# Decays by pair of heads, one-pass squares and a longer due time for the substitution in a gated-delta layer

## The chip, the cores and the metric

The kernel runs on one core of one Trainium2 chip. The metric is the device time of one launch in microseconds (us); the time shown is the median of three runs.

## The reference

One inference step through two layers of a streaming encoder, for 1024 prompt frames and 64 frames of a running stream (1088 columns in all, 17 chunks of 64), width 1024, all in fp32. Layer 1 (a gated convolution beside banded attention) is not touched. Layer 2 is a gated DeltaNet with 8 heads of 128: a projection, a causal convolution of width 4 with SiLU on q, k and v, and per head and chunk:

```python
def gdn_chunk(S, q, k, v, g, beta):
    gc = jnp.cumsum(g, axis=1)
    decay = jnp.exp(jnp.where(incl, gct[..., :, None] - gct[..., None, :], -jnp.inf))
    a = jnp.where(strict, bt[..., :, None] * kk * decay, 0.0)     # kk = k k^T
    sol = lax.linalg.triangular_solve(a + eye, rhs, left_side=True, lower=True, unit_diagonal=True)
    u = sol[..., :HD_C] - sol[..., HD_C:] @ S
    o = (q * jnp.exp(gc)) @ S + (q k^T * decay) @ u
    S_new = jnp.exp(g_last) * S + k_dec^T @ u
```

q and k are first divided by their norm (`l2norm`, a sum of squares over 128). S goes from chunk to chunk, so the 17 chunks of a head are a chain. The output is normed per head, multiplied by silu(z) and projected.

## The kernel before

**Tiling.** A projection takes one weight tile of 128 output columns (`w`) and runs over three groups of columns (384, 384, 320). Every fp32 product is made of three matmuls in fp32r, from weights and inputs that were split into a high and a low part: `pjt<-hhi,wlo`, `pjt<-hhi,whi`, `pjt<-hlo,whi`, for each of eight slices of the contraction. Below, a "projection row" is one such matmul. ACT and DVE split the weights (`whi` L164, `wlo` L165) as they come by DMA (`wf`, on SP's queue).

**Layer 2.** The heads go in four pairs p = 0 to 3. `conv_tile` projects and convolves six tiles for a pair (q, k, v). The 17 chunks of a pair come in three batches of 6, 6 and 5 chunks; the twelve batches n = 3p + b each go through five streams of work:

- `prep` (function `prepare`): the decays `E` (`decay`: DVE L902 spreads the running sums `gc` into `An`, a matmul `tr<-An,cst` adds them up across lanes, DVE L907 subtracts, ACT L908 and L909 make exp(-|x|)); transposes of k and q (`tr<-cst,kq`), of which ACT takes squares chunk by chunk with an accumulator (`junk`, L948), ACT copies k (`kt`, L950) and DVE scales it (`kd`, L951); POOL takes the root of the sums (`rk`, L956 and L957), scales `kt` (L961) and masks `E` into `KQD` (L962); matmuls `tr<-kq`, from which DVE makes `An` (L970) and `KQD` (L971); and the diagonal blocks `Af`, which SP's queue writes to DRAM.
- `sub` (`substitute`): SP's queue reads them back as `AL`, and POOL inverts 48 blocks of 16x16 row by row (`px` L996, `AL` L997); SP's queue writes them to DRAM again.
- `inv` (`join`): read as `Xf`, masked by POOL into `X` (L1025), transposed by DVE into `XT` (L1026), and joined to inverses of 64x64 by small matmuls (`tr<-XT,Cb` first, then `tr<-M,X`, `tr<-XT,An`, `tr<-M,X`).
- `wy` (`solve`): `tr<-cst,vt`, `tr<-BD,kt`, `tr<-vr,BD`.
- `scan`: chunk by chunk `ks<-S,kq`, DVE makes `us` (L1145), `su<-us,kd`, DVE makes the new `S` (two instructions, L1159), and `tr<-us,KQD` gives the output, which DVE adds up (`o`, L1114) and ACT squares (L1118). For each four chunks `finish` takes POOL's root (`so`, L1173 and L1174), scales `o` (DVE L1176) and transposes it (`tr<-cst,o`).

All these matmuls and transposes write PSUM tiles named `tr` (two banks), `ks` and `su`. A `tr` bank is free again when its last reader on ACT or DVE is through.

**What sets the order.** TensorE's order is written by the kernel itself: `Order` has a clock of its own, which each matmul moves on by its columns. A stream is a generator; `yield w` says that it is due again w ns later, and of the streams that are due the one with the lowest rank goes on: `scan` 1, `wy` 1.3, `inv` 1.5, `sub` 1.6, `prep` 2, the stream `main` with all projections 5. So projections fill what the others leave. `yield "name"` waits for a stream's end: `main` waits for `scan2` before pair 2 and for `scan5` before pair 3 (two buffers of `kq`), and for the last batch's transposed outputs before tile 6 of the gate. DVE, ACT, POOL and SP are ordered by the compiler's scheduler. Every engine then takes its own list strictly in order.

Of the kernel before, what the change touches and what calls it, by code (L numbers as in the profile page):

```python
# [7 lines left out]
F32 = mybir.dt.float32  # L8
# [7 lines left out]
P = 128  # L16
# [91 lines left out]
class Net:  # L108
# [650 lines left out]
    def odd(self):  # L759
# [16 lines left out]
        def conv(ti, dst, g, ps, prev):  # L776
# [20 lines left out]
            if half:  # L797
                th = k1.tile([P, GMAX + 3], F32, name="th", tag="raw", bufs=3)[:, :n]
                act.activation(ch(th), o, AF.Tanh)
                dve.scalar_tensor_tensor(o, ch(th), 1.0, o, ALU.add, ALU.mult)  # L800
            else:
                act.activation(o, o, AF.Silu)
# [29 lines left out]
        def gate(ti):  # L832
            w = self.take()
            for g, (t0, n) in enumerate(GROUPS):
# [9 lines left out]
                nc.sync.dma_start(oo, od[:, ti, t0:t0 + n])  # L844
                zs = (gp if ti == 7 else k1).tile([P, GMAX + 3], F32, name="zs", tag="raw", bufs=3)[:, :n]
                act.activation(zs, ps[:, :n], AF.Silu)
# [50 lines left out]

        def decay(e, gx, p, c0, m):

            sh = [P, m, 64]  # L900
            gcb = G["gc"][:, p, c0:c0 + m].unsqueeze(2).broadcast_to(sh)
            dve.tensor_tensor(gx, gcb, cst[:, C_ID64:C_ID64 + 64].unsqueeze(1).broadcast_to(sh), ALU.mult)  # L902
            yield 900
            ps = pst("tr")[:, :64 * m]
            self.mm(ps, cst[:, C_BD:C_BD + P], gx.rearrange("p c j -> p (c j)"))
            ps = ps.rearrange("p (c j) -> p c j", j=64)
            dve.tensor_tensor(ps, ps, gcb, ALU.subtract)  # L907
            act.activation(e, ps, AF.Abs)  # L908
            act.activation(e, e, AF.Exp, scale=-1.0)  # L909

# [10 lines left out]
        def prepare(p, b):  # L921
# [10 lines left out]

            E, An, KQD = bt("E", 64), bt("An", 64, 2), bt("KQD", 64, 3)
            yield from decay(E, An, p, c0, nb)
            if b == 0:
                yield 4000
            kd, kt = bt("kd", P, 3), bt("kt", P, 2)
            ss = self.kp.tile([P, 2, NBM], F32, name="ss", tag="ss", bufs=2)[:, :, :nb]
            junk = self.kp.tile([P, P], F32, name="junk", tag="junk", bufs=1)
            for i0 in range(0, nb, 4):  # L940
                m = min(4, nb - i0)
                for a in range(2):
                    ps = pst("tr").rearrange("p (c j) -> p c j", j=P)
                    for i in range(m):
                        c = c0 + i0 + i
                        self.tr(ps[:, i, :], kq[:, a, c].rearrange("p q t -> p (q t)"))
                    for i in range(m):
                        act.activation(junk, ps[:, i, :], AF.Square, accum_out=ss[:, a, i0 + i:i0 + i + 1])  # L948
                    if a == 0:
                        act.copy(out=kt[:, i0:i0 + m, :], in_=ps[:, :m, :])  # L950
                        dve.tensor_tensor(kd[:, i0:i0 + m, :], ps[:, :m, :],  # L951
                                          dec[:, p, c0 + i0:c0 + i0 + m].unsqueeze(2).broadcast_to([P, m, P]), ALU.mult)
                    yield 2160
            sT, sA, kap, rk, eq = (small(x) for x in ("sT", "sA", "kap", "rk", "eq"))
# [29 lines left out]
        def substitute(p, b):  # L984
# [7 lines left out]
            for j in range(1, 15):  # L992
# [5 lines left out]
                if j % 2 == 0:  # L998
                    yield 700
            pool.memset(AL.rearrange("p r j -> p (r j)")[:, 0:256:17], 1.0)  # L1000
# [186 lines left out]

        def add_pair(p):
            for b in range(NB):
                n = NB * p + b  # L1190
# [6 lines left out]
                order.add(f"sub{n}", 1.6, substitute(p, b), [f"prep{n}"] + after("sub", n - 1))  # L1197
                order.add(f"prep{n}", 2, prepare(p, b), ["gates"] + after("prep", n - 1) + after("wy", n - 2) + after("scan", n - 3))

# [133 lines left out]
```

## Time and profile before

| | |
|---|---|
| median of 3 runs | 1436.92 us (1434.3 to 1437.56) |
| profiled execution | 1433.82 us, its span 1432.0 us |
| PE busy | 1362.8 us, 95% of the span |
| DVE, ACT, POOL busy | 58%, 49%, 19% |
| mean granted TensorE clock | 0.986 |

An engine's busy time is the union of its instructions. A busy PE is not a PE at its peak, since a matmul's row is longer than the distance to the next one. In the views a row such as `PE tr L119 <- ACT E L908` means that TensorE's next instruction, which writes or reads a tile `tr`, waited for ACT's instruction at line 908. L119 is the line of the helper that records all matmuls, L124 that of all transposes.

### The profile page before, as it was taken

Reading aid. Unit: us, or ns where it says so; the run is one execution under the profiler, and the core shown is the slowest. Engines: PE = TensorE matmul, PEld = TensorE weight load, DVE = VectorE, ACT = ScalarE, POOL = GpSimd, SP = SyncE. Lnnn points to the kernel's source line nnn. Section 1 sums busy time; section 2 is a strip of 40 time slices with the busy share of each in tenths; the row PEclk is TensorE's granted clock in tenths of the full one; section 3 lists DMA queues with packets and bytes.
Section 4 is the critical chain, followed back from the end, with each engine's and each line's share of the span. In section 5 each row is a group of like instructions: output and inputs, shape, how many; then the busy total and the mean of one; then the engine's idle time right before and its main releaser. Section 6 shows DMA issues by size and latency. Waiting matters only on the chain. (4 is left out here: it accounts for less than half of the span.)

```text
span 1432.0 us, 27829 instructions
## 1 busy us (share of the span) xinstructions
PE 1362.8 (95%) x10600; PEld 1227.5 (86%) x10600; DVE 834.1 (58%) x2232; ACT 696.7 (49%) x1792; POOL 276.0 (19%) x578
## 2 busy tenths in 40 slices
PE   8999999999999999999999988999999989999996
PEld 6989998998999899888987777787878777889995
DVE  7675247237425754778786756667665654433555
ACT  7543345144334455675545463546454635333752
POOL 4000000000100014322151325212412151300122
PEclk9999999999999999999999999999999999999998
DMA  8403111210211164451220212112211232336753
GB/s 267 140 17 90 57 53 45 88 53 22 77 58 53 61 229 151 158 186 38 60 40 19 46 37 52 16 44 45 47 15 42 68 68 60 91 103 206 235 197 123
DMA packets 106917, 123.77 MB, mean 86 GB/s; under 512 B 34512, under 2 KB 73880, under 8 KB 106784
## 3 DMA queue, kind: packets, MB, share of 16 engines
q1 hardware_dynamic: 78992, 99.86, 23.7%
q10 hardware_dynamic: 27792, 22.15, 4.9%
q8 instruction: 83, 1.36, 0.4%
q14 instruction: 50, 0.41, 0.1%
HBM read 95.26 MB, written 29.86 MB: 87 GB/s over the span
## 5 line engine op out<-in xcount | busy, mean ns | idle before, releaser
L119 PE MATMUL pjt<-hhi,wlo 128*128 128x384 f32 (+1 forms) x1768 | 613.9, 347 | 2.3 <-DVE wlo L165 2.3
L119 PE MATMUL pjt<-hhi,whi 128*128 128x384 f32 (+1 forms) x1768 | 582.5, 330 | 8.1 <-ACT whi L164 4.7
L119 PE MATMUL pjt<-hlo,whi 128*128 128x384 f32 (+1 forms) x1768 | 575.2, 329 | 1.1 <-DVE hlo L417 1.1
L119 PEld LDWEIGHTS pjt<-hhi,wlo 128*128 128x128 f32 x1768 | 335.9, 190 | 26.0 <-issue 11.6
L119 PEld LDWEIGHTS pjt<-hhi,whi 128*128 128x128 f32 x1768 | 336.6, 190 | 13.8 <-ACT whi L164 6.0
L119 PEld LDWEIGHTS pjt<-hlo,whi 128*128 128x128 f32 x1768 | 334.5, 190 | 2.0 <-DVE hlo L417 2.0
L165 DVE TENSOR_TENSOR wlo<-wf,whi 128x512 fp32r<-128x512 f32 x222 | 151.8, 709 | 167.6 <-ACT whi L164 162.7
L164 ACT CAST whi<-wf 128x512 fp32r<-128x512 f32 x222 | 130.2, 619 | 163.3 <-PE pjt L119 116.0
L638 ACT ACTIVATE pr<-pr,mx 128x640 f32<-128x640 f32 (+5 forms) x72 | 50.9, 707 | 89.4 <-DVE mx L637 88.8
L796 DVE SCALAR_TENSOR_TENSOR kq<-pjt,par,kq 128x384 f32<-128x384 f32 (+2 forms) x144 | 71.7, 498 | 3.0
L374 POOL TENSOR_TENSOR sqa<-sqa,sq 128x384 f32<-128x384 f32 (+1 forms) x36 | 39.1, 1086 | 137.1 <-ACT sq L371 137.0
L635 DVE CUSTOM_DVE_ANT_0 pr<-sc,bias 128x640 f32<-128x640 f32 (+5 forms) x72 | 48.0, 666 | 26.7 <-PE sc L119 25.9
L599 POOL MEMSET bias<- 64x64 f32 x8 | 1.4, 173 | 320.5 <-DMA bias<-Gd 227.5
L1159 DVE SCALAR_TENSOR_TENSOR S<-S,egl,su 128x128 f32<-128x128 f32 x128 | 39.8, 342 | 37.3 <-PE su L119 37.2
L948 ACT ACTIVATE junk<-tr 128x128 f32<-128x128 f32 x136 | 37.7, 277 | 33.4 <-PE tr L124 27.0
L996 POOL TENSOR_TENSOR px<-AL 48x14 f32<-48x14 f32 (+6 forms) x168 | 45.4, 270 | 33.4 <-DMA AL<-Sd 21.6
L1118 ACT ACTIVATE junk<-o 128x128 f32<-128x128 f32 x68 | 21.0, 309 | 61.4 <-DVE o L1114 55.1
L997 POOL TENSOR_TENSOR AL<-AL,px 48x14 f32<-48x14 f32 (+6 forms) x168 | 47.7, 284 | 11.7
L124 PE MATMUL pt<-cst,pr 128*128 128x128 f32 (+1 forms) x280 | 43.3, 270 | 4.3 <-DVE pr L640 2.9
L119 PE MATMUL pjt<-mhi,whi 128*128 128x384 f32 x128 | 43.0, 336 | 1.2 <-ACT whi L164 1.2
L119 PE MATMUL pjt<-mhi,wlo 128*128 128x384 f32 x128 | 43.0, 336 | 0.1
L119 PE MATMUL ks<-S,kq 128*64 128x128 f32 x512 | 43.0, 288 | 0.0
(252 smaller groups left out, 2107.1 us busy)
## 6 DMA issues: line engine op xcount, KB each, us to landing
wf<-in_w_in SPq DMA_DIRECT2D x128, 256.0 KB, 3.3
wf<-in_w_out SPq DMA_DIRECT2D x96, 256.0 KB, 2.9
mf<-mixd SPq DMA_DIRECT2D x31, 192.0 KB, 4.2
x<-in_x SPq DMA_DIRECT2D x8, 384.0 KB, 6.7
xg<-in_x SPq DMA_DIRECT2D x2, 1536.0 KB
xd<-xg SPq DMA_DIRECT2D x2, 1536.0 KB, 7.3
od<-o ACTq DMA_DIRECT2D x12, 256.0 KB, 2.1
oo<-od SPq DMA_DIRECT2D x16, 192.0 KB
```

Of the source, the lines that this page charges most:

```text
L119: return self.pe.matmul(out, lhsT=lhsT, rhs=rhs, start=start, stop=stop, **k)
L124: return self.pe.transpose(out, in_, self.ident[0:k, 0:k])
L164: self.act.copy(out=hi, in_=x)
L165: (eng or self.dve).tensor_tensor(lo, x, hi.bitcast(F32), ALU.subtract)
L374: pool.tensor_tensor(acc, acc, sq, ALU.add)
L635: dve.tensor_tensor_reduce(out=cut(pr[0:nq, :nk]), in0=sc[0:nq, :nk // nw, :nw], in1=cut(b["bias"][a][0:nq, j0:j0 + nk]), scale=1.0, scala ...
L638: act.activation(pr[0:nq, :nk], pr[0:nq, :nk], AF.Exp, bias=mx[0:nq, 1:2], scale=1.0, accum_out=mx[0:nq, 2:3])
L796: dve.scalar_tensor_tensor(oi, ch(ps[:, i0 + j + 1:i0 + j + 1 + m]), cw[j], oi, ALU.mult, ALU.add)
L948: act.activation(junk, ps[:, i, :], AF.Square, accum_out=ss[:, a, i0 + i:i0 + i + 1])
L996: pool.tensor_tensor(t, AL[:, j + 1:16, j:j + 1].broadcast_to([lanes, m, w]), x.broadcast_to([lanes, m, w]), ALU.mult)
L997: pool.tensor_tensor(o, o, t, ALU.add)
L1159: dve.scalar_tensor_tensor(Sn[:, q, :], S[:, q, :], egl[:, q, p, c:c + 1], su[q], ALU.mult, ALU.add)
```

## The change

Three things, all in layer 2:

- `decays(p)` replaces `decay` per batch: one stream `dec{p}` makes the decays of all 17 chunks of a pair into one tile `E` (128x1088). The three spreads, the three matmuls and the three subtractions stay, but the spreads and the subtractions write `E` in SBUF, and ACT's two functions run once over the whole tile (`Abs`, then `Exp`). `prep{n}` now waits for `dec{p}`; `dec{p}` waits for the gates and for the last `prep` of the pair before.
- The squares: ACT squares up to four chunks at once, in place in the PSUM bank and behind the copy `kt` and the scaling `kd`, and DVE adds them up with a reduce into `ss`.
- `substitute` yields 1250 instead of 700 after every second row, seven times in a batch.

To make room, the tag `raw` has two buffers where it had three (but in the last tile of the gate).

```diff
-                th = k1.tile([P, GMAX + 3], F32, name="th", tag="raw", bufs=3)[:, :n]
+                th = k1.tile([P, GMAX + 3], F32, name="th", tag="raw", bufs=2)[:, :n]
...
-                zs = (gp if ti == 7 else k1).tile([P, GMAX + 3], F32, name="zs", tag="raw", bufs=3)[:, :n]
+                zs = (gp if ti == 7 else k1).tile([P, GMAX + 3], F32, name="zs", tag="raw", bufs=3 if ti == 7 else 2)[:, :n]
...
-        def decay(e, gx, p, c0, m):
...
-            dve.tensor_tensor(ps, ps, gcb, ALU.subtract)
-            act.activation(e, ps, AF.Abs)
-            act.activation(e, e, AF.Exp, scale=-1.0)
+        def decays(p):
+
+            E = G["E"] = self.kp.tile([P, NCH, 64], F32, name="E", tag="E")
+            gcb = G["gc"][:, p].unsqueeze(2).broadcast_to([P, NCH, 64])
+            for c0, m in BATCHES:
+                c = slice(c0, c0 + m)
+                dve.tensor_tensor(E[:, c], gcb[:, c], cst[:, C_ID64:C_ID64 + 64].unsqueeze(1).broadcast_to([P, m, 64]), ALU.mult)
+            yield 1500
+            for c0, m in BATCHES:
+                c = slice(c0, c0 + m)
+                ps = pst("tr")[:, :64 * m]
+                self.mm(ps, cst[:, C_BD:C_BD + P], E[:, c].rearrange("p c j -> p (c j)"))
+                dve.tensor_tensor(E[:, c], ps.rearrange("p (c j) -> p c j", j=64), gcb[:, c], ALU.subtract)
+                yield 300
+            act.activation(E, E, AF.Abs)
+            act.activation(E, E, AF.Exp, scale=-1.0)
...
-            E, An, KQD = bt("E", 64), bt("An", 64, 2), bt("KQD", 64, 3)
-            yield from decay(E, An, p, c0, nb)
+            E, An, KQD = G["E"][:, c0:c0 + nb], bt("An", 64, 2), bt("KQD", 64, 3)
...
-                    for i in range(m):
-                        act.activation(junk, ps[:, i, :], AF.Square, accum_out=ss[:, a, i0 + i:i0 + i + 1])
                     if a == 0:
                         act.copy(out=kt[:, i0:i0 + m, :], in_=ps[:, :m, :])
                         dve.tensor_tensor(kd[:, i0:i0 + m, :], ps[:, :m, :],
                                           dec[:, p, c0 + i0:c0 + i0 + m].unsqueeze(2).broadcast_to([P, m, P]), ALU.mult)
+                    act.activation(ps[:, :m, :], ps[:, :m, :], AF.Square)
+                    dve.tensor_reduce(out=ss[:, a, i0:i0 + m], in_=ps[:, :m, :], axis=mybir.AxisListType.X, op=ALU.add)
...
-                    yield 700
+                    yield 1250
...
+            order.add(f"dec{p}", 2, decays(p), ["gates"] + ([f"prep{NB * p - 1}"] if p else []))
...
-                order.add(f"prep{n}", 2, prepare(p, b), ["gates"] + after("prep", n - 1) + after("wy", n - 2) + after("scan", n - 3))
+                order.add(f"prep{n}", 2, prepare(p, b), [f"dec{p}"] + after("prep", n - 1) + after("wy", n - 2) + after("scan", n - 3))
```

The matmuls are the same in number and size; their order on TensorE changes from the start of layer 2's decays to the end of its scans.

**TensorE, decays.** In batch 8 (last of pair 2) the decays' matmul stood ahead of four transposes and an output pair of the scan, which takes the `tr` bank that the decays' matmul had filled:

```order
L119 MATMUL pjt<-hlo_6042,whi 128x384
L119 MATMUL tr<-An,cst 128x384
L124 MATMUL tr<-cst,kq 128x128 x4
L119 MATMUL tr<-us,KQD 64x128 x2
L119 MATMUL pjt<-hhi_6041,wlo 128x384
L119 MATMUL pjt<-hhi_6041,whi 128x384
L119 MATMUL pjt<-hlo_6042,whi 128x384
```

(These rows are of batch 10, the same pattern; in batch 8 the output pair is the first of its scan, `tr<-vt,KQD`.) Now the three matmuls of a pair stand together. For pair 3:

```order
L119 MATMUL ks<-S,kq 64x128 x4
L119 MATMUL tr<-M,X 32x16 x20
L119 MATMUL tr<-E,cst 128x384
L119 MATMUL su<-us,kd 128x128 x2
L119 MATMUL tr<-E,cst 128x384
L119 MATMUL tr<-XT,An 32x32 x10
L119 MATMUL tr<-E,cst 128x320
L119 MATMUL tr<-us,KQD 64x128 x2
L119 MATMUL pjt<-hhi_6041,wlo 128x384
```

Twelve single matmuls in twelve places have become four groups of three; the transposes `tr<-cst,kq` of all batches now stand without a decays' matmul beside them.

**ACT, the squares of pair 3's second batch.** Before, from the exponential of its decays to the square of the scan's last output of pair 2 (`junk,so`):

```order
L909 ACTIVATE E<-E 128x384
L783 ACTIVATE vt<-pjt,par 128x6x64
L802 ACT_TABLE_LOAD
L802 ACTIVATE vt<-vt 128x6x64
L948 ACTIVATE junk,ss<-tr 128x128 x5
L783 ACTIVATE vt<-pjt,par 128x6x64
L948 ACTIVATE junk,ss<-tr 128x128
L950 COPY kt<-tr 128x256
L1184 ACTIVATE o_12776<-tr,par 128x256 x2
L1185 DMA od<-o_12776 128x2x256
L948 ACTIVATE junk,ss<-tr 128x128 x2
L1118 ACTIVATE junk,so<-o_12959 128x128
```

Now (lines have moved by two; L953 is the square of up to four chunks):

```order
L953 ACTIVATE tr<-tr 128x512
L950 COPY kt<-tr 128x256
L783 ACTIVATE vt<-pjt,par 128x6x64
L953 ACTIVATE tr<-tr 128x256
L1120 ACTIVATE junk,so<-o_12774 128x128
L953 ACTIVATE tr<-tr 128x256
L1149 ACTIVATE qs<-ks,egc 128x128
L802 ACTIVATE vt<-vt 128x5x64
L802 ACTIVATE vt<-vt 128x6x64
L1169 DMA out_S<-S 128x256
L1120 ACTIVATE junk,so<-o_13019 128x128
```

Between the start of the listing and the last output's square stood eight squares of one chunk, a table load and a SiLU; now three squares of up to four chunks and two SiLUs, and no exponential.

**TensorE, the last chunk of the last pair.** Before, behind its `su` (the row above these) and up to the outputs' transposes:

```order
L119 MATMUL pjt<-hhi_6891,wlo 128x320
L119 MATMUL pjt<-hhi_6891,whi 128x320
L119 MATMUL pjt<-hlo_6892,whi 128x320
L119 MATMUL pjt<-hhi_6891,wlo 128x320
L119 MATMUL pjt<-hhi_6891,whi 128x320
L119 MATMUL pjt<-hlo_6892,whi 128x320
L119 MATMUL pjt<-hhi_6891,wlo 128x320
L119 MATMUL pjt<-hhi_6891,whi 128x320
L119 MATMUL pjt<-hlo_6892,whi 128x320
L119 MATMUL tr<-us,KQD 64x128 x2
L119 MATMUL pjt<-hhi_6891,wlo 128x320
L124 MATMUL tr<-cst,o_14599 128x128 x4
```

Now:

```order
L119 MATMUL pjt<-hhi_6891,wlo 128x320
L119 MATMUL tr<-us,KQD 64x128 x2
L119 MATMUL ks<-S,kq 64x128 x4
L119 MATMUL su<-us,kd 128x128 x2
L119 MATMUL tr<-us,KQD 64x128 x2
L124 MATMUL tr<-cst,o_14556 128x128 x4
L124 MATMUL tr<-cst,o_14731 128x128
```

The projection rows that stood inside the last chunk now stand earlier, ahead of the last batch's join (18 rows ahead of its `tr<-XT,Cb`, where there were 6). The last chunk of pair 0 has lost its filling in the same way.

More of the change, by code (lines that the diff above doesn't have):

```diff
@@ L896, in gates @@
             yield 1500
-        def decay(e, gx, p, c0, m):
[L900 to L909, printed above, removed]
+        def decays(p):
[13 more added lines that the diff above has]
+            act.activation(E, E, AF.Exp, scale=-1.0)
         Z = {}
@@ L938, in prepare @@
             ss = self.kp.tile([P, 2, NBM], F32, name="ss", tag="ss", bufs=2)[:, :, :nb]
-            junk = self.kp.tile([P, P], F32, name="junk", tag="junk", bufs=1)
             for i0 in range(0, nb, 4):
```

## Prediction

> **What bounds the kernel now.** First the totals of the page, then the span cut into three stages (columns: length, busy time of PE, its weight loads, DVE, ACT, POOL, with the instructions in brackets, granted clock, DMA share, GB/s).
>
> ```profile
> span 1432.0 us, 27829 instructions
> PE 1362.8 (95%) x10600; PEld 1227.5 (86%) x10600; DVE 834.1 (58%) x2232; ACT 696.7 (49%) x1792; POOL 276.0 (19%) x578
> ...
> 0.00:700.00 700.00, 681.72 (x4488) 638.48 (x4489) 404.91 (x1010) 341.69 (x755) 75.27 (x85) 1.00 0.30 97
> 700.00:1296.00 596.00, 560.13 (x5401) 471.95 (x5400) 362.25 (x1112) 290.98 (x907) 174.67 (x468) 0.98 0.21 50
> 1296.00:1432.00 136.00, 120.95 (x715) 117.10 (x713) 66.93 (x111) 64.03 (x131) 26.09 (x25) 0.97 0.58 193
> ```
>
> TensorE bounds every stage; DVE and ACT are busy for 61% and 49% of the middle one, where the whole change lies. That stage has 596.0 - 560.1 = 35.9 us without a matmul and a clock of 0.98. TensorE's work is the same after the change, so the time can move only by TensorE's waits, by its clock, and by what an empty stretch adds. Hence the second view, TensorE's waits from 700 to 1296 (us in total, times, longest):
>
> ```profile
> PE tr L119 <- ACT E L908: 8.9, 5, 2.6
> PE tr L124 <- DVE o L1176: 7.6, 2, 5.4
> PE tr L119 <- DVE XT L1026: 5.8, 2, 3.1
> PE tr L119 <- DVE KQD L971: 3.3, 7, 1.2
> PE tr L124 <- DVE kd L951: 1.8, 1, 1.8
> PE tr L119 <- ACT vr L1084: 1.6, 2, 1.1
> PE tr L124 <- DVE o L1114: 1.5, 3, 0.8
> PE tr L119 <- DVE kd L951: 1.5, 2, 1.3
> PE tr L119 <- ACT M L1055: 1.2, 1, 1.2
> PE su L119 <- DVE us L1145: 1.0, 2, 0.5
> PE tr L119 <- DVE pjt L790: 0.8, 1, 0.8
> PE tr L119 <- ACT M L1037: 0.3, 1, 0.3
> PE tr L124 <- ACT junk L948: 0.3, 1, 0.3
> PE tr L119 <- ACT junk L948: 0.2, 1, 0.2
> ```
>
> The three longest kinds are the decays (an output pair of the scan waits until ACT has read the decays' bank), one late output, and the substitution's result `XT`. Third, the instructions around the long ones, and the clock behind them:
>
> ```profile
> 876.78 0.58 PE L119 MATMUL tr<-XT,Cb 32*32 32x16 f32 x48 [3.13 <-DVE XT L1026]
> ...
> 1020.70 0.58 PE L119 MATMUL tr<-XT,Cb 32*32 32x16 f32 x48 [2.62 <-DVE XT L1026]
> ...
> 1044.77 0.46 PE L119 MATMUL tr<-vt,KQD 64*64 64x128 f32 x4 [2.54 <-ACT E L908]
> ...
> 878.00:882.00 4.00, 4.00 (x61) 3.52 (x60) 3.21 (x10) 0.52 (x1) 3.00 (x13) 0.60 0.02 6
> 1021.00:1028.00 7.00, 7.00 (x121) 6.28 (x110) 4.37 (x12) 0.82 (x2) 5.48 (x20) 0.51 0.02 4
> 1045.00:1049.00 4.00, 4.00 (x23) 2.96 (x20) 1.32 (x4) 3.12 (x8) 0.86 (x1) 0.57 0.00 0
> 1157.60:1164.60 7.00, 6.34 (x32) 5.17 (x34) 3.38 (x12) 0.99 (x3) 1.79 (x8) 0.51 0.32 89
> ```
>
> Behind these three, and behind the longest at 1158, TensorE runs at about half its clock for 3 to 7 us while it is busy. The loss is length times what the clock lacks: 4 x 0.40 + 7 x 0.49 + 4 x 0.43 + 7 x 0.49 = 1.6 + 3.4 + 1.7 + 3.4 = 10.1 us.
>
> **The change part by part.** The prices, from the groups of the middle stage (columns behind the bar: busy time, mean ns of one, idle before and its releaser):
>
> ```profile
> L948 ACT ACTIVATE junk<-tr 128x128 f32<-128x128 f32 x136 | 37.7, 277 | 33.4 <-PE tr L124 27.0 <-DMA out_convC<-ends 3.3 <-ACT junk L948 0.8
> ...
> L948 ACT ACTIVATION_READ_ACCUMULATOR junk<-tr 128x1 f32 x136 | 26.9, 198 | 0.0
> ...
> L909 ACT ACT_TABLE_LOAD x10 | 12.8, 1283 | 0.2
> ...
> L951 DVE TENSOR_TENSOR kd<-tr,dec 128x512 f32<-128x512 f32 x12 | 8.3, 689 | 8.3 <-ACT kt L950 8.1
> ...
> L950 ACT COPY kt<-tr 128x512 f32<-128x512 f32 x12 | 7.0, 581 | 0.0
> ...
> L907 DVE TENSOR_TENSOR tr<-tr,gc 128x384 f32<-128x384 f32 x7 | 3.9, 559 | 0.0
> ```
>
> *Decays.* The scan's outputs no longer share their `tr` bank with an exponential: the bank is free after DVE's subtraction (559 ns), and eight of the twelve places where the decays' matmul stood among scan rows are gone. All five waits go: -8.9. What is late next at those places is DVE's subtraction itself, where two decays' matmuls and two more users of the two banks follow closely (the order of pairs 1 to 3). Two subtractions in series are 1.1 us and the rows between are worth about half of that, so 0 to 1.1 per pair; I take 0.7, three times: +2. The exponential over 1088 columns is first needed behind all transposes of the next `prep`, which hide it (by the row of `kt` at 581 for 512, two functions of some 1.2 us); table loads fall from 36 to 22 in the list, 14 x 1.283 = 18 us of ACT, off the path.
>
> *Squares.* ACT loses 136 x (277 + 198) = 65 us of instruction time and gains 48 squares (24 of 512 columns, 16 of 256, 8 of 128, some 34 full ones). A square in PSUM has no row here; by the copy of the same shape (581) that is 20 us. DVE gains as many reduces; a reduce has no row either; by `kd`, the same shape out of the same bank (689), it is 23 us, off the path unless it stands before the scan's `us` or `S`. In DVE's list 18 reduces have one of these in the next two rows. If none delays the scan the cost is 0; if each holds it for its whole 0.69 us, 12 us. The scan's rows have mostly six to nine projections between them, more than an S takes, so I take 2, near the lower end. What the shorter ACT queue gives is best seen at the longest wait:
>
> ```profile
> 1142.58 0.29 DVE L1114 TENSOR_TENSOR o<-tr,qs 128x128 f32<-128x128 f32 x1
> ...
> 1152.22 0.31 ACT L1118 ACTIVATE junk<-o 128x128 f32<-128x128 f32 x1
> ...
> 1157.24 0.55 POOL L1174 TENSOR_TENSOR so<-so,root 128x1 f32<-128x1 f32 x1
> ```
>
> The output stood ready for 9.6 us until ACT had its square behind eight squares, a table load and a SiLU, and POOL's root came another 5 us later behind that batch's `rk` and `kt`, which wait for the same squares. Between that output and its last transpose stand 54 projection rows now (52 before), some 10 us; by ACT's list as it is now the square comes in the first half of that, so this wait goes: -5.4. The small waits for `kd`, `vr` and `M` (1.8 + 1.6 + 1.5 + 1.2 = 6.1) come from the same full queue; between none and all I take half: -3.
>
> *Substitution.* It moves the joins behind more projections: between the last `tr<-kq` and `tr<-XT,Cb` stand 150 projection rows for batch 6, where there were 111. Batch 3 has no more (84, after 96), but POOL now takes its 28 steps without the next batch's `rk` and `kt` among them. What those cost shows in batch 6 (POOL's list):
>
> ```profile
> 1004.85 0.24 POOL L956 TENSOR_SCALAR rk<-ss 128x6 f32<-128x6 f32 x1 [2.11 <-ACT junk L948]
> ...
> 1005.41 1.35 POOL L957 TENSOR_TENSOR rk<-rk,root 128x6 f32<-128x6 f32 x1
> ...
> 1007.70 1.46 POOL L961 TENSOR_TENSOR kt<-kt,kap 128x768 f32<-128x768 f32 x1
> ```
>
> 2.11 + 0.24 + 1.35 + 1.46 = 5.2 us, more than batch 3 was late (3.13). Both waits go: -5.8. Batch 9 has `rk`, `kt`, `KQD` and two roots among its steps and one weight load ahead of `Xf` on SP's queue: it can come late by 0 to 2, +1. Longer streams also run out of projections: the last chunks of pairs 0 and 3 have none left around `su`. There TensorE waits for `us`, some 0.6 us each: +1.2. The other ten batches had slack, so there the pause only shifts rows.
>
> *Buffers.* `raw` with two: a `zs` is used again two groups later, 48 projection rows on, and no wait of TensorE's list above goes back to one; 0.
>
> *Clock.* With those four waits their half-clock stretches go: -10.1.
>
> *The order as a whole.* Half of TensorE's list is dealt anew, and with it the waits that have none of these causes: 3.3 + 1.5 + 1.0 + 0.8 + 0.3 + 0.3 + 0.2 = 7.4. They can vanish or double; I let them double: +7.4.
>
> Sum: -8.9 - 5.4 - 3 - 5.8 - 10.1 = -33.2; +2 + 2 + 1 + 1.2 + 7.4 = +13.6; together -19.6, so the span goes from 1432.0 to 1412.4 and the profiled execution from 1433.8 to 1414.2. That execution is 3.1 under the median of the runs, so the median goes from 1436.9 to about 1417.
>
> [...]
>
> **The rivals.**
>
> (a) *The half clock stays*, or falls elsewhere. For it speaks one more wait for `E`, as long as the others, with a full clock behind it:
>
> ```profile
> 1142.09 0.43 PE L119 MATMUL tr<-us,KQD 64*64 64x128 f32 x4 [2.59 <-ACT E L908]
> ...
> 1142.00:1150.00 8.00, 7.91 (x52) 7.51 (x53) 2.98 (x9) 7.00 (x21) 3.89 (x14) 1.00 0.08 13
> ```
>
> So the clock doesn't follow from a wait's length alone. All else as above: 1417 + 10 = 1427. Against it: four of the five longest waits have a half-clock stretch behind them.
>
> (b) *The order brings new long waits.* Ten places with other neighbours; if two thirds of the 33 come back (22 in place of 7.4), the time is 1432. For it: the streams' other due times are as they were, and DVE and ACT, which their scheduler orders without TensorE's real lateness, still stand in line behind a late `XT` or SiLU.
>
> (c) *The change doesn't free the bank.* Copy, scaling, square and reduce now follow each other on two engines, 581 + 689 + 581 + 689 = 2.5 us and three handovers, where it was 4 x 475 + 581 + 689 = 3.2 and one. `kd` waited for `kt` for (8.1 us in 12) 0.7 us each; with two more handovers of that size the bank is held for 4.6 in place of 3.9 us. If the 24 such groups each cost TensorE 0.8 us, the 20 are used up: 1437.
>
> (d) *Slower: the reduces hold up the scan.* In DVE's list a reduce before `S` waits for ACT's square, and that for what ACT has ahead of it. If the 18 reduces next to `us` or `S` wait behind one table load and one SiLU (1.28 + 0.5 us) each, TensorE loses 32 us: 1449 - 2 = 1447. It turns from gain to loss at 20 / 18 = 1.1 us each. Against it: table loads are fewer by 14, and ACT is busy for half of the stage.
>
> (e) *More is gained*: the redealt waits don't double and all small waits go, 1437 - 33 - 3 + 6 = 1407.
>
> **How the numbers follow.** My forecast has 0.55, (a) 0.07, (b) 0.17, (c) 0.07, (d) 0.10, (e) 0.04. Within 0.2%, about what a measurement of this kernel can tell from no change, is 1434.0 to 1439.8. Faster: 0.55 + 0.07 + 0.17 + 0.04 = 0.83; same 0.07; slower 0.10. The forecast's own range is 1405 to 1427, from the bounds of its terms; with (b) at the upper end and (e) at the lower one 1402 to 1434 leaves out (c), (d) and little more.
>
> **What the profile of the changed kernel would show.** If I am right, TensorE's waits have no row for `E`; none for `XT` over 2 us; none over 3 us for `o`; fewer windows at half clock (one, at the end of the scans, stays); 22 table loads; ACT's busy time lower by 50 to 65 us and DVE's higher by 20 to 25; TensorE's busy time in the middle stage lower by some 10 us, by the clock. I'd be wrong if new long waits for DVE (`ss`, `S`, `us`) stand where the old ones were, or if the stage is shorter but the end, where weights come by DMA at 193 GB/s, gives it back.

## The result, and the profile after

The changed kernel takes 1452.28 us (median of four runs, 1449.95 to 1454.63) against 1435.61 for the kernel before: ratio 1.0116, 95% interval 1.0086 to 1.0146. It is 1.2% slower where 1.4% faster was forecast, and the time lies outside the range. The totals of the page of the changed kernel, and its three stages (columns as before; the middle stage now ends at 1316):

```profile
span 1452.8 us, 27612 instructions
PE 1375.6 (95%) x10600; PEld 1238.5 (85%) x10600; DVE 851.9 (59%) x2280; ACT 655.7 (45%) x1538; POOL 275.5 (19%) x578
...
0.00:700.00 700.00, 678.55 (x4473) 634.95 (x4474) 404.12 (x1006) 340.61 (x752) 75.47 (x85) 1.00 0.30 97
700.00:1316.00 616.00, 575.57 (x5430) 486.23 (x5429) 381.35 (x1165) 251.23 (x656) 173.99 (x468) 0.96 0.20 49
1316.00:1452.80 136.80, 121.44 (x701) 117.37 (x699) 66.41 (x110) 63.82 (x130) 26.04 (x25) 0.95 0.57 190
```

The last transpose of an output, which ends the scans, has moved from 1291.3 to 1308.0:

```profile
1291.31 0.45 PE L124 MATMUL tr<-cst,o 128*128 128x128 f32 x1 [2.23 <-DVE o L1176]
```

```profile
1308.01 0.45 PE L124 MATMUL tr<-cst,o 128*128 128x128 f32 x1 [0.34 <-DVE o L1178]
```

So 16.7 of the 20.8 us by which the profiled spans differ are lost up to the end of the scans and 4.1 behind it, where the clock is 0.95 in place of 0.97. (The profiled execution of the changed kernel was the slowest of its four; the medians differ by 16.7 us.) ACT has 41 us less to do and DVE 18 more, each a little less than forecast (50 to 65 and 20 to 25), and neither is the bound. TensorE stands without a matmul for 1452.8 - 1375.6 = 77.2 us, where it was 69.2. At a mean granted clock of 0.975 (0.986 before) it lacks 1452.8 x 0.025 = 36.3 us of clock, where it was 1432.0 x 0.014 = 20.0 (with a clock of three places, each is good to 0.7 us). So 8.0 us more are waited and 16.3 us more are lost to the clock; 3.5 us less of the rest, as it would be if a wait inside a half-clock stretch is counted in both. Of the 8.0 us 4.6 lie in the middle stage and 3.2 ahead of it.

TensorE's waits in the middle stage (700 to 1316; lines have moved by two):

```profile
PE tr L119 <- DVE KQD L973: 17.8, 7, 5.4
PE tr L119 <- ACT vt L1095: 4.6, 2, 4.0
PE su L119 <- DVE us L1147: 2.9, 5, 1.2
PE pjt L119 <- DVE pjt L790: 1.9, 2, 1.2
PE tr L124 <- DVE o L1178: 1.8, 2, 1.4
PE tr L119 <- DVE o L1116: 1.4, 1, 1.4
PE tr L119 <- DVE XT L1028: 1.4, 1, 1.4
PE ks L119 <- DVE S L1161: 1.2, 2, 1.0
...
PE tr L119 <- DVE E L910: 0.5, 1, 0.5
```

The old list was headed by ACT's `E` (8.9), the late output (7.6) and `XT` (5.8): those are down to nothing, 1.8 and 1.4. At the head now stands `KQD`, 3.3 before: TensorE needs a `tr` bank that still holds the products `tr<-kq`, because DVE hasn't yet made `An` and `KQD` from them. `vt` is a wait of 4.0 us that had no row at all. Three of the `KQD` waits, and the clock of the stretches that begin with them (mean granted clock is the number behind the last bracket):

```profile
803.86 0.57 PE L119 MATMUL tr<-XT,An 32*32 32x32 f32 x24 [2.87 <-DVE KQD L973]
...
1084.94 0.76 PE L119 MATMUL tr<-XT,An 32*32 32x32 f32 x21 [2.92 <-DVE KQD L973]
...
1174.35 1.12 PE L119 MATMUL tr<-kq 128*64 128x128 f32 x8 [5.43 <-DVE KQD L973]
...
803.00:815.00 12.00, 11.14 (x93) 8.31 (x93) 7.00 (x28) 2.80 (x11) 1.21 (x2) 0.57 0.04 5
1084.00:1095.00 11.00, 10.06 (x89) 7.71 (x89) 6.89 (x28) 2.88 (x10) 1.21 (x2) 0.53 0.04 5
1173.00:1181.00 8.00, 6.65 (x32) 6.35 (x33) 5.07 (x20) 0.98 (x3) 4.30 (x16) 0.57 0.06 8
```

Two waits of 2.9 us are each followed by some 10 us at half clock, which lacks 12 x 0.43 = 5.2 and 11 x 0.47 = 5.2 us: more than the waits themselves. Behind the 5.43 us it is 8 x 0.43 = 3.4 us, less than the wait.

What DVE and POOL did before 1174 (their lists in order; in the bracket the idle time before and what ended it):

```profile
1167.99 0.24 DVE L960 TENSOR_TENSOR sT<-beta,rk 128x6 f32<-128x6 f32 x1 [2.04 <-POOL rk L959]
...
1169.66 3.45 DVE L1178 TENSOR_SCALAR o<-o,so 128x128 f32<-128x128 f32 x4 [0.83 <-POOL so L1176]
1173.03 0.85 DVE L972 SCALAR_TENSOR_TENSOR An<-tr,sA,E 128x64 f32<-128x64 f32 x4
1173.80 0.41 DVE L973 TENSOR_TENSOR KQD<-tr,KQD 128x256 f32<-128x256 f32 x1
...
1169.85 1.46 POOL L963 TENSOR_TENSOR kt<-kt,kap 128x768 f32<-128x768 f32 x1
1171.28 0.28 POOL L998 TENSOR_TENSOR px<-AL 48x56 f32<-48x56 f32 x1
1171.53 0.85 POOL L964 TENSOR_TENSOR KQD<-E,cst 128x320 f32<-128x320 f32 x1
```

The bank was written by 1167.8. DVE waited 2.04 us for POOL's `rk`, which stood among the rows of the substitution, then 0.83 us for an output's root, and then took 3.45 us for four scalings, while POOL ran its two large products; the first of the four alone took 2.81 us (last section). `An` and `KQD`, which free the bank, stood behind that in DVE's list.

### The profile page after: what moved, and what is told of

Read it like the earlier page. It is cut to its first block, busy times and chain, and to the rows that moved or that the text cites. A ratio compares the mean times of both kernels' runs of the same rounds, so it can differ in the third digit from the quotient of the medians.

```text
span 1452.8 us, 27612 instructions
## 1 busy us (share of the span) xinstructions
PE 1375.6 (95%) x10600; PEld 1238.5 (85%) x10600; DVE 851.9 (59%) x2280; ACT 655.7 (45%) x1538; POOL 275.5 (19%) x578
## 5 line engine op out<-in xcount | busy, mean ns | idle before, releaser
L119 PE MATMUL pjt<-hhi,wlo 128*128 128x384 f32 (+1 forms) x1768 | 617.1, 349 | 2.9 <-DVE wlo L165 2.9
L119 PE MATMUL pjt<-hhi,whi 128*128 128x384 f32 (+1 forms) x1768 | 585.4, 331 | 12.7 <-ACT whi L164 4.9
L119 PE MATMUL pjt<-hlo,whi 128*128 128x384 f32 (+1 forms) x1768 | 577.4, 330 | 1.1 <-DVE hlo L417 1.1
L119 PEld LDWEIGHTS pjt<-hhi,wlo 128*128 128x128 f32 x1768 | 338.0, 191 | 26.5 <-issue 11.9
L119 PEld LDWEIGHTS pjt<-hhi,whi 128*128 128x128 f32 x1768 | 338.9, 192 | 19.3 <-ACT whi L164 6.2
L119 PEld LDWEIGHTS pjt<-hlo,whi 128*128 128x128 f32 x1768 | 336.9, 191 | 2.0 <-DVE hlo L417 2.0
L796 DVE SCALAR_TENSOR_TENSOR kq<-pjt,par,kq 128x384 f32<-128x384 f32 (+2 forms) x144 | 71.5, 497 | 2.8
L635 DVE CUSTOM_DVE_ANT_0 pr<-sc,bias 128x640 f32<-128x640 f32 (+5 forms) x72 | 48.0, 666 | 26.8 <-PE sc L119 25.9
L802 ACT ACTIVATE kq<-kq 128x384 f32<-128x384 f32 (+1 forms) x36 | 18.2, 505 | 60.6 <-DVE kq L796 60.1
L119 PE MATMUL ks<-S,kq 128*64 128x128 f32 x512 | 43.8, 290 | 1.2 <-DVE S L1161 1.2
L119 PE MATMUL pjt<-mhi,whi 128*128 128x384 f32 x128 | 43.1, 337 | 1.8 <-ACT whi L164 1.8
L119 PE MATMUL pjt<-mhi,wlo 128*128 128x384 f32 x128 | 43.1, 337 | 0.2
```

Source lines behind the costliest of these rows:

```text
L119: return self.pe.matmul(out, lhsT=lhsT, rhs=rhs, start=start, stop=stop, **k)
L635: dve.tensor_tensor_reduce(out=cut(pr[0:nq, :nk]), in0=sc[0:nq, :nk // nw, :nw], in1=cut(b["bias"][a][0:nq, j0:j0 + nk]), scale=1.0, scala ...
L796: dve.scalar_tensor_tensor(oi, ch(ps[:, i0 + j + 1:i0 + j + 1 + m]), cw[j], oi, ALU.mult, ALU.add)
```

## The experiments

Each kernel ran beside the kernel before, on one chip. "Without a matmul" is the profiled span less PE's busy time, "clock" the span times what the mean granted clock lacks of 1, both in us. Each ratio goes by the runs of the kernel before that were made with it (medians 1435.2 to 1437.8), and need not be the quotient of the medians. Leads and pauses are numbers of `yield`, in ns of the order's clock.

| kernel | median us | ratio, 95% interval | span | without a matmul | clock |
|---|---|---|---|---|---|
| before | 1435.61 | 1 | 1432.0 | 69.2 | 20.0 |
| changed | 1452.28 | 1.0116, 1.0086 to 1.0146 | 1452.8 | 77.2 | 36.3 |
| squares alone | 1441.93 | 1.0028, 1.0009 to 1.0047 | 1441.3 | 72.7 | 25.9 |
| pause 1250 alone | 1446.65 | 1.0071, 1.0041 to 1.0101 | 1449.3 | 79.8 | 27.5 |
| two `raw` buffers alone | 1438.37 | 0.9997, 0.9974 to 1.0020 | 1439.4 | 72.1 | 24.5 |
| decays (and buffers) | 1446.24 | 1.0054, 1.0028 to 1.0080 | 1444.6 | 72.4 | 31.8 |
| changed, pause 700 | 1453.76 | 1.0118, 1.0076 to 1.0159 | 1451.1 | 78.5 | 29.0 |
| changed, squares by chunk | 1457.15 | 1.0134, 1.0098 to 1.0170 | 1453.2 | 77.5 | 37.8 |
| changed, scaling on ACT | 1452.43 | 1.0103, 1.0071 to 1.0135 | 1450.1 | 78.0 | 29.0 |
| before, pause 760 | 1444.21 | 1.0042, 1.0018 to 1.0065 | 1435.7 | 69.5 | 23.0 |
| before, output's lead 9400 | 1447.02 | 1.0076, 1.0051 to 1.0102 | 1442.2 | 77.0 | 23.1 |
| before, pause 1250 in first batches | 1440.91 | 1.0033, 1.0010 to 1.0057 | 1442.0 | 67.5 | 33.2 |
| changed, output's lead 9400 | 1447.12 | 1.0057, 1.0026 to 1.0089 | 1449.6 | 74.6 | 34.8 |
| changed, lead of k and q 800 | 1445.62 | 1.0071, 1.0049 to 1.0093 | 1442.8 | 67.7 | 33.2 |
| changed, lead 900 | 1434.08 | 0.9964, 0.9934 to 0.9994 | 1436.0 | 65.8 | 28.7 |
| the same, measured again | 1431.31 | 0.9964, 0.9944 to 0.9985 | 1429.7 | 63.1 | 25.7 |
| changed, lead 1200 | 1445.33 | 1.0077, 1.0047 to 1.0107 | 1443.4 | 71.5 | 28.9 |
| before, lead 900 | 1436.60 | 0.9993, 0.9973 to 1.0013 | 1437.0 | 68.8 | 25.9 |
| changed, lead 900, output's 9400 | 1436.29 | 0.9999, 0.9978 to 1.0019 | 1444.0 | 70.8 | 33.2 |
| before, lead 900, output's 9400 | 1440.08 | 1.0025, 1.0007 to 1.0043 | 1439.6 | 69.9 | 28.8 |

In each row the span less the last two columns is 1338 to 1344 us. TensorE's work is the same in all twenty; what differs is its waits and its clock.

**The parts, one at a time.** Each edit alone on the kernel before. The squares:

```diff
-                    for i in range(m):
-                        act.activation(junk, ps[:, i, :], AF.Square, accum_out=ss[:, a, i0 + i:i0 + i + 1])
...
+                    act.activation(ps[:, :m, :], ps[:, :m, :], AF.Square)
+                    dve.tensor_reduce(out=ss[:, a, i0:i0 + m], in_=ps[:, :m, :], axis=mybir.AxisListType.X, op=ALU.add)
```

> The kernel before with the new squares alone: TensorE's order is the same as before, row for row. Theory A (DVE pays for the squares: its 48 reduces stand ahead of what frees the banks and of the scan): slower by 8 to 15 us, with TensorE's new waits for DVE's KQD already here. Theory B (the dealt order, not the squares, costs the time): faster by 4 to 10 us, since ACT's queue is shorter and the wait of 5.4 us at 1158 goes.

The pause:

```diff
-                    yield 700
+                    yield 1250
```

> The kernel before with 1250 in place of 700 alone. Theory B1 (the longer pause pushes the joins of one batch onto the next batch's preparation and the scan, where DVE serves all three in one list): slower by 5 to 15 us, with waits for KQD. Theory B2 (the pause is good, the decays' order is bad): faster by 5 to 10 us, the two waits for XT gone and no new ones of more than 2 us.

The buffers:

```diff
-                th = k1.tile([P, GMAX + 3], F32, name="th", tag="raw", bufs=3)[:, :n]
+                th = k1.tile([P, GMAX + 3], F32, name="th", tag="raw", bufs=2)[:, :n]
```

> The kernel before with two buffers of raw alone; every engine's order is the same as before. Theory C (the third buffer was needed in the first tiles of layer 2, where TensorE now waits 3.7 us at 698): slower by 4 to 6 us. Rival: that wait comes from the decays of all three batches being spread ahead of the convolution on DVE; then within 1 us of before.

And `decays(p)` in place of `decay`, with the two buffers that it needs, squares and pause as before:

```diff
+            order.add(f"dec{p}", 2, decays(p), ["gates"] + ([f"prep{NB * p - 1}"] if p else []))
...
+            E, An, KQD = G["E"][:, c0:c0 + nb], bt("An", 64, 2), bt("KQD", 64, 3)
```

> The kernel before with the decays by pair (and two buffers of raw, without which they don't fit): pause 700 and squares by chunk as before. Theory A: 5 to 10 us faster (the waits for E go, 8.9 us, and little comes). Theory B2: slower by 5 to 15 us. Theory C: 4 to 6 us less gain than without the buffers' loss.

The buffers cost nothing that shows. Each of the three others is slower by itself, by 0.28, 0.71 and 0.54%. TensorE's longest waits in the middle stage, first with the squares, then with the pause, then with the decays:

```profile
PE tr L119 <- DVE XT L1025: 12.0, 4, 4.3
PE tr L119 <- ACT E L908: 6.6, 5, 2.3
...
PE tr L124 <- DVE o L1175: 2.2, 1, 2.2
```

```profile
PE su L119 <- DVE us L1145: 11.8, 5, 5.4
PE tr L119 <- ACT E L908: 10.6, 7, 3.5
PE tr L124 <- DVE o L1176: 4.1, 1, 4.1
```

```profile
PE tr L119 <- DVE XT L1029: 14.5, 3, 5.6
PE tr L119 <- ACT vr L1087: 5.4, 3, 3.2
```

Each part does what it was made to do. With the squares alone no output is late by more than 2.2 us; with the pause alone `XT` has no row; with the decays alone ACT's `E` has none. And each brings waits that weren't there or were shorter: `XT` twice as long, the scan's `us`, `XT` again with `vr` (and, with the decays, 4.3 us for a convolution's `kq` at 698). With the squares TensorE's order is that of before, row for row; what was dealt anew there is DVE's, ACT's and POOL's lists.

**Two parts, and DVE's queue at 1174.** The changed kernel with the old pause:

```diff
-                    yield 1250
+                    yield 700
```

> The changed kernel with the stream's pause left at 700: decays by pair, squares of four chunks, two raw buffers. Its order on TensorE is that of the run with the decays alone, word for word; only ScalarE and VectorE differ, by the squares. Theory A (the squares have a price of their own, about 4 us, as on the old order: VectorE reads 18 more banks and releases others later): 1450 us, ratio 1.008, KQD and XT waits somewhat longer than with the decays alone, half clock about 70 us. Theory B (the parts have no price of their own; each new arrangement of queues gets its own waits by chance): the time can fall to either side of the decays alone, 1436 to 1455 us. Theory D (the squares are a gain once the exponential sits once per pair, since ScalarE has 17 us less to do): 1440 us or less.

The changed kernel with the squares by chunk (the first diff, reversed):

> The changed kernel with the squares chunk by chunk on ScalarE with its accumulation, as before; decays by pair, pause 1250, two raw buffers. Its order on TensorE is the changed kernel's, word for word. Theory A (the squares cost about 4 us wherever they are): 1448 us, ratio 1.009; the KQD waits lose some of their 17.8 us, the half clock a few us of its 74. Theory B (the waits belong to the order on TensorE, and the squares neither make nor cure them): 1452 us, the waits for KQD at 804, 889, 1016, 1085 and 1174 us stand where they stood. Theory D: slower than the changed kernel, 1456 us.

The changed kernel with the outputs scaled on ACT:

```diff
-                dve.tensor_scalar(o4[:, i, :], o4[:, i, :], fa[:, i:i + 1], None, ALU.mult)
+                act.activation(o4[:, i, :], o4[:, i, :], AF.Copy, scale=fa[:, i:i + 1])
```

> The changed kernel with the scaling of the outputs (o times so, 68 instructions) on ScalarE in place of VectorE. The order on TensorE is the changed kernel's, word for word. Theory A (the wait of 5.4 us at 1174 for KQD is VectorE's queue: the scaling waits for GpSimd's root and then runs at a quarter of its speed beside GpSimd's large products, while An and KQD stand behind it): that wait falls below 2 us, the half-clock window behind it goes, the KQD sum falls from 17.8 to about 12 us, and the time falls by 5.4 + 3.4 = 9 us at that place, to 1443 us; ScalarE's busy time rises by 20 to 30 us and its own waits for so may take 2 us back. Theory B (the bank is claimed too early by the order itself, whatever VectorE does): the wait stays over 3 us and the time at 1450 to 1455 us.

Adding the squares on an equal TensorE order costs 0.28% on the old one and about 0.6% on that of the decays (1.0054 to 1.0118), and on the changed one, if anything, gives 0.2% (1.0134 to 1.0116, which the intervals don't resolve). The pause, 0.71% alone, adds nothing to the other two (1.0118 to 1.0116). So no part has one price, and neither the forecast of a fixed 4 us for the squares nor that of a gain held. With the squares by chunk three of the changed kernel's five long waits for `KQD` stand (2.87, 2.92 and 6.03 us); the two of 2.5 and 2.67 us at 889 and 1016 are gone, and the waits for `us` rise from 2.9 to 6.2. The scaling on ACT, on the same order of TensorE:

```profile
1172.99 0.66 PE L119 MATMUL tr<-kq 128*64 128x128 f32 x8 [2.06 <-DVE KQD L973]
...
1173.00:1181.00 8.00, 8.00 (x56) 7.79 (x57) 6.92 (x19) 4.79 (x14) 7.14 (x19) 1.00 0.19 40
...
PE tr L119 <- DVE KQD L973: 13.4, 7, 2.9
PE su L119 <- DVE us L1147: 5.2, 6, 2.0
```

The wait falls from 5.4 to 2.06 us, the half clock behind it is gone (1.00 where it was 0.57), and the `KQD` sum falls from 17.8 to 13.4. That is the mechanism at this place, much as expected (below 2 us and about 12). But the kernel takes 1452.43 us and not 1443: 7.3 us of clock come back in the profiled execution (36.3 to 29.0), none of the waits do (77.2 to 78.0), and the medians are equal. Other waits have grown: `us` went from 2.9 to 5.2, `E` from 0.5 to 2.0, `XT` from 1.4 to 2.5.

**The same instructions, dealt otherwise.** Here no instruction is added or taken away; a due time moves, and with it the places of TensorE's rows. Such an order of the same instructions is called a deal below. On the kernel before, the pause by 60 ns:

```diff
-                    yield 700
+                    yield 760
```

> The kernel before with the stream's pause at 760 in place of 700, and nothing else: no instruction is added, removed or changed, but some 800 rows of TensorE's order move by a few places. Theory B (the old order is a lucky one among many like it, and any other deal of the small work among the projections brings waits of 2.5 to 6 us that the old one hasn't): slower by 0.2 to 0.8%, 1439 to 1448 us, with one or more new waits over 2.5 us and a half clock of 45 to 60 us. Theory A (each part of the change has its own price, the order by itself none): within 0.2% of before, 1433 to 1439 us, with the same waits for E, XT and o.

and the output's lead in `finish`, the time between the scaling of the outputs and their transposes:

```diff
-            yield 9000
+            yield 9400
```

> The kernel before with the output's lead at 9400 in place of 9000 and nothing else: a second deal of the same instructions, one that moves other rows (the outputs' transposes) than the pause does. Theory B (any other deal of the old order costs 0.2 to 0.8%): 1439 to 1448 us. Theory A (a deal by itself costs nothing; the pause of 760 did something of its own): 1433 to 1439 us.

and the longer pause for the first batch of each pair alone, four batches, at two of which TensorE waited for `XT` (3.13 and 2.62 us; the text below counts three):

```diff
-                    yield 700
+                    yield 700 if b else 1250
```

> The kernel before with the pause of 1250 for the first batch of each pair alone, the three at whose XT it waited 2.5, 1.8 and 1.0 us. Theory A: the XT waits and their half clock go and nothing else comes, 1426 to 1432 us. Theory B: they go, and the deal that follows brings waits elsewhere: 1438 to 1448 us.

All three are slower, by 0.42, 0.76 and 0.33%: as much as the parts of the change. In the third the waits for `XT` are gone and TensorE waits no longer than before (67.5 us against 69.2); there it is the clock that costs (33.2 against 20.0). In the second the longest waits are these:

```profile
PE tr L119 <- ACT E L908: 8.7, 5, 3.3
PE tr L119 <- ACT vr L1084: 8.6, 3, 6.2
PE tr L124 <- DVE o L1176: 5.9, 1, 5.9
```

A wait of 6.2 us for `vr`, where the longest was 1.1, has come from nothing but another order. (The profiled execution of the first was the lowest of its ten, so its row in the table flatters it.) The output's lead on the changed kernel:

> The changed kernel with the output's lead at 9400 in place of 9000 and nothing else. Theory B1 (the new order is one draw from the same lot as the old one's neighbours, and an unlucky one): a new deal is likelier better than worse, 1440 to 1452 us. Theory B2 (the parts together put a price of about 10 us on every order, above what a deal costs): 1448 to 1458 us, whatever moves.

The same edit that cost the kernel before 0.76% takes the changed one from 1.0116 to 1.0057.

**The lead behind the k and q products.** If `KQD` waits because the bank is claimed again too soon, more projections between the products and the next claim should help (in `prepare`, behind L973):

```diff
-                yield 510
+                yield 900
```

> The changed kernel with 900 in place of 510 behind each group of k and q products, so that 390 more of projections stand between them and the next claim on their bank. Theory A (the waits for KQD are a lead that is too short): KQD falls from 17.8 us to under 5, with 20 us of its half clock: 1432 to 1440 us. Theory B (waits are moved, not taken away: VectorE's queue is as full at the next claim): KQD falls, others of 2.5 to 6 us come in at XT, us, vt or S, and the time stays at 1446 to 1458 us.

It did more than any other edit: faster than the kernel before. What was open then was whether the lead would have helped the kernel before as well, whether it was the lead or a lucky deal (an order that happens to have few long waits), and whether it would stand in a second measurement:

> The changed kernel with 900 in place of 510 behind the k and q products, measured again in five rounds. If the first measurement holds: ratio 0.994 to 0.999 to before, 1429 to 1436 us. If it was one chip's and one hour's chance: 1.000 or more.

> The kernel before with 900 in place of 510 behind the k and q products and nothing of the change. Theory L1 (the longer lead is a gain of its own): faster than before, 1425 to 1433 us. Theory L2 (the old order waited 3.3 us for KQD in all, so the lead has nothing to give there, and a deal costs 0.3 to 0.8% as the other four did): 1440 to 1448 us, and the change is worth 0.5 to 1% at equal lead.

> The changed kernel with 1200 in place of 510 there. Theory A (the lead cures the change's waits for KQD): KQD stays under 6 us, where 510 had 17.8, and the time stays at 1428 to 1440 us. Theory B (900 was a lucky deal among orders that lie at 1440 to 1457 us): 1442 to 1455 us.

> The changed kernel with 900 there, and the output's lead at 9400 in place of 9000, the edit that cost the kernel before 0.76% and gave the changed kernel 0.6%. Theory A (the lead cures, a deal adds a few us either way): 1430 to 1442 us, below the 1447 us of the same deal with 510. Theory B (900 was luck): 1445 us or more.

> The changed kernel with 800 in place of 510 there, an order between that of 510 and that of 900. Theory A (the lead): KQD waits of 5 to 12 us in all, the time between 1434 and 1452, about 1441 us. Theory B (each deal for itself, no trend in the lead): anywhere from 1431 to 1457 us, the KQD sum not falling in step with the lead.

> The kernel before with 900 there and the output's lead at 9400. If the change is worth 0.2 to 0.3% at equal deals with this lead (0.9964 against 0.9993 at 9000): 1439 to 1443 us against the 1436.3 of the changed kernel. If the change is worth nothing and each deal stands for itself: anywhere from 1436 to 1448 us.

The second measurement of 900 (totals, middle stage, waits):

```profile
span 1429.7 us, 27610 instructions
PE 1366.6 (96%) x10600; PEld 1234.0 (86%) x10600; DVE 846.4 (59%) x2280; ACT 655.7 (46%) x1538; POOL 274.6 (19%) x578
...
700.00:1296.00 596.00, 569.52 (x5448) 484.03 (x5449) 378.19 (x1171) 251.77 (x657) 172.47 (x468) 0.97 0.21 51
...
PE su L119 <- DVE us L1147: 6.9, 6, 2.0
PE tr L119 <- DVE XT L1028: 5.0, 2, 2.9
PE tr L119 <- DVE KQD L973: 4.2, 3, 2.9
PE tr L119 <- ACT vr L1086: 3.6, 3, 2.3
```

and the `KQD` row at 800 and at 1200:

```profile
PE tr L119 <- DVE KQD L973: 11.0, 7, 2.9
```

```profile
PE tr L119 <- DVE KQD L973: 11.1, 7, 2.5
```

The gain of 900 stands: 0.9964 twice. No wait in the middle stage is longer than 2.9 us. But it isn't a matter of the lead alone: `KQD` goes 17.8, 11.0, 4.2, 11.1 us over 510, 800, 900 and 1200, and the time 1452, 1446, 1431 to 1434, 1445. 1200 gives no more than 800. So in these four the waits for `KQD` and the time go together, while neither goes steadily with the lead; elsewhere they don't (with the old pause `KQD` is 7.1 us and the time 1453.76). 900 is a good deal; whether the longer lead has a part of its own in that isn't shown. For the kernel before, 900 neither gains nor costs. With both leads varied, the ratios to the kernel before are:

| lead of k and q, output's lead | instructions of before | changed instructions |
|---|---|---|
| 510, 9000 | 1 | 1.0116 |
| 510, 9400 | 1.0076 | 1.0057 |
| 900, 9000 | 0.9993 | 0.9964 |
| 900, 9400 | 1.0025 | 0.9999 |

At three of the four settings the change is 0.2 to 0.3% ahead, and in each of the three the two intervals overlap; in the fourth, the change as given, it is 1.2% behind. Equal leads are not an equal order, since the change moves rows of its own. Over the deals of this study, six other than the given one of the old instructions average 1.0040 (the three above with moved due times, pause 1250, and the two with 900), and seven of the changed ones 1.0057 (as given, pause 700, output's lead 9400, lead 800, 900, 1200, and 900 with 9400). The averages lie closer together than the deals do (0.9964 to 1.0118), and the kernel before has a good deal: of its six neighbours none is measurably faster.

## Why the prediction was wrong

Its steps on what goes were right, its steps on what comes were not.

- *`E`, -8.9*: right. 0.5 us is left, for DVE's subtraction, where +2 was allowed. Alone it works too: no ACT `E` row with the decays.
- *Late output, -5.4*: right. The longest is 1.4. The squares do it alone (2.2).
- *`XT`, -5.8*: right in the main, 1.4 is left, at batch 0 and not at batch 9, for which +1 was taken. The pause does it alone; but with the squares or the decays alone `XT` rose to 12.0 and 14.5, so the wait isn't a fixed cost that one part owns.
- *Small waits, -3*: about right. `kd` and the squares' `junk` have no row, and rows for `vr` and `M` of 1.1 us and less stand for the 6.1.
- *Prices of the new instructions*: right. The reduce of 128x512 was taken at 689 ns and the square at 581; they measure:

```profile
L954 DVE TENSOR_REDUCE ss<-tr 128x4 f32<-128x512 f32 x24 | 16.4, 684 | 2.1 <-ACT tr L953 2.1
...
L953 ACT ACTIVATE tr<-tr 128x512 f32<-128x512 f32 x24 | 14.1, 586 | 10.4 <-PE tr L124 5.1 <-DVE kd L951 4.2 <-DVE pjt L790 0.9
```

- *Reduces beside the scan, +2, and the last chunks of pairs 0 and 3, +1.2*: about right. `us` went from 1.0 to 2.9 (1.2 and 0.6 of it in those two chunks) and `S` came to 1.2. Rival (d), slower because of the reduces, is right in its sign and wrong in its mechanism; rival (c), banks held longer, shows with 0.4 us of waits for `ss`.
- *Buffers, 0*: right.
- *The order as a whole, +7.4*: this failed. The waits without a cause of their own were let double, from 7.4 to 14.8. `KQD` alone went to 17.8, `vt` added 4.6, and a wait of 3.7 us for a convolution came at 698, just ahead of the middle stage (`PE pjt L119 <- DVE kq L796`; the decays alone have it too, with 4.3). The step looked at where each edit moved rows and took all else as small because it was small in the old order. It was small in an order that the runs show to be a good one: with the old instructions, three shifts of a due time cost 0.3 to 0.8%, two with new long waits (`XT` 4.9, `vr` 6.2 us), the third by the clock.
- *The clock, -10.1*: this failed with it, and is the larger part in us. The sum took the old waits' half clock off and put none on the new ones. In the changed kernel two waits of 2.9 us drew 5 us each, and four of 2.5 to 5.4 us, at 778, 889, 1016 and 1174, drew 1.7 to 3.4 each. The profiled execution lost 16.3 us more to the clock where it was to lose 10.1 less; TensorE's busy time in the middle stage rose by 15.4 where it was to fall by some 10. By the prediction's own sum the waits were to fall by 9.5 (-23.1 + 13.6); they rose by 8.0.

Rival (b), "the order brings new long waits", came nearest to the mechanism, with a chance of 0.17, but its price was too small: it let 22 of the 33 us come back, which ends at 1432 and still below no change. The time measured is 35 us above the forecast, so more than the whole 33 was given back.

Shown is that the named waits go, that others come, that more is lost to the clock (mostly, but not always, behind a long wait), and that another deal of the changed instructions alone is worth as much as the change (1.0116 to 0.9964). At 1174 it is shown what DVE's queue did. Which of the moved rows make the given deal worse than the others isn't shown, nor is a price of the change itself: with both leads varied it ran from about -0.3 to +1.2%.

## What to carry to other kernels

Where a written order weaves small work into a bound engine's stream, a change that re-deals it is a new draw, and the removed waits are no forecast of the sum: first move a due time by some per cent in the unchanged kernel and see what a deal is worth, here up to 0.8%. Price a wait of TensorE with the half clock behind it, which in the changed kernel was 1.7 to 5 us for six waits of 2.5 to 5.4 us (a rough price, see below). And judge a change over several deals, not one: the same changed instructions ran from 0.9964 to 1.0118.

## What the runs showed of the hardware

In the changed kernel a scaling on DVE that reads and writes SBUF took up to 2.81 us while POOL worked, where the median of the 68 is 0.28. Four scalings took 3.45 us at 1169 (above); the same four in the kernel before, with POOL idle beside them, took:

```profile
1138.16 0.87 DVE L1176 TENSOR_SCALAR o<-o,so 128x128 f32<-128x128 f32 x4
```

They weren't all slowed: one of them made the difference. The 68 scalings of the changed kernel (shortest, median and longest in ns):

```profile
L1178 DVE TENSOR_SCALAR o<-o,so x68: 271/280/2807, 807.6 to 1307.6; 128x128 f32<-128x128 f32 x68
```

The longest, of 2.81 us, is the first of the four. It began at 1169.66, when POOL was at work; POOL's instructions followed one another without a break, and it ended 0.09 us behind POOL's `KQD` (1171.53 + 0.85). At 854.62 two scalings took 1.68 us, the first of them 1.49, beside POOL's `kt` of 1.47 us that began at 854.56. Both long ones ended within 0.1 us of POOL's product; why, no run here shows. Beside two POOL instructions for `so`, of 0.26 and 0.84 us, four scalings at 894.12 took 0.86 us. In the kernel before no scaling took over 0.32 us.

Half the clock follows some waits and not others, and not by their length alone: 2.87 and 2.92 us were followed by 10 us at half clock, and 2.06 us, in the kernel with the scaling on ACT, by none. One program run twice (lead 900) had much the same long waits, and 28.7 and 25.7 us of clock lost. Its wait of 2.33 us for ACT's `vr`, which ended at 1062.25 in the first execution and at 1057.69 in the second, had the half clock in the one (0.50 over 6.8 us) and not in the other. Nor is the stretch as long as the wait: 5.43 us drew 6.8 us of half clock, and in the kernel before with the pause of 1250 in the first batches the longest stretch stands behind 1.29 us, at a join:

```profile
1203.04 0.59 PE L119 MATMUL tr<-XT,Cb 32*32 32x16 f32 x48 [1.29 <-DVE kd L951]
...
1204.80:1218.50 13.70, 12.91 (x144) 9.38 (x133) 6.99 (x23) 4.02 (x11) 2.69 (x3) 0.50 0.22 66
```

The two stretches of 10 us at 803 and 1084 stand at joins as well (`tr<-XT,An`), and with the output's lead at 9400 a wait of 1.68 us at that place, at 1086, is followed by 10.2 us too. So four stretches of some 10 to 14 us stand at joins, behind waits of 1.29 to 2.92 us; whether what TensorE runs behind a wait counts beside the wait itself, no run here was made to test, and a price of the clock per wait stays rough.
